# Two-layer hybrid streaming encoder: score rows of the sample requests gathered 64 wide, and the instruction order worked out with another model

## The chip, the cores and the metric

The kernel runs on one core of one Trainium2 chip, in one launch. The metric is the device time in microseconds of an execution. A core has five engines with a queue each, worked off in order: TensorE (PE in the profile; its weight loads are the rows PEld), VectorE (DVE), ScalarE (ACT), GpSimd (POOL) and SyncE (SP), which here only issues transfers.

## The reference, cut to what matters

Two layers, each with three mixers side by side (latent attention A, a gated recurrence B, differential attention C), sigmoid gates, an output projection and a gated MLP. The tokens are one prompt of 512 and eight sample requests of 16 tokens each, every request with a cache of 512 past keys. The change is in mixer C for the sample requests:

```python
s = einsum('bqhjd,bkhjd->bjhqk', qd, dk_all) * DF_SCALE   # j = 0, 1: two score maps per head
p = softmax(where(chunk_mask, s, NEG), axis=-1)
a = p[:, 0] - lam * p[:, 1]                                # 16 tokens x 8 heads, 528 keys
o_c = einsum('bhqk,bkhd->bqhd', a, dv_all)
o_c = rms(o_c, diff_norm_g) * (1 - lam_init)
```

Per request there are 2 maps x 8 heads x 16 tokens = 256 score rows over 512 cached and 16 new keys.

## The kernel before, in words

All is float32; the large products are split in a high and a low part of type fp32r and take three matmuls (`mm3`, L119 to L123). The 640 tokens are five tiles of 128. In a layer four Python generators are stepped in an order written out by hand, the string `ORDER`: `stream_a`, `stream_b`, `stream_c` for the mixers and `stream_g` for the gates. After them come the merge of the branches, the output projection and the MLP (up-projection, convolution, down-projection), without generators.

The stepping gives each instruction a place in the program. The Tile library then makes each engine's queue out of it: it runs the program on a model of the machine and hands an engine, when that model says it is free, the earliest instruction that the model says is ready. So work of one stream fills gaps of another: projections of `stream_g` and `stream_b` stand between the short steps of the attention and the recurrence. Which model is used is an argument of `tile.TileContext` in `build` (L1389). On the chip an engine keeps the order it was given.

Mixer C for the samples is one step per request b (eight per layer, sixteen in all):

- `c_probs(b)`. Four tiles of keys `kc` and four of values `vc` are loaded. For each block of two heads (`blk`, 0 to 3) four transposes (L831) and a copy give the keys `kT` with the features on the partitions, 128 x 512. `Qz` holds the queries of a block spread out with zeros, 32 columns per map j (two heads x 16 tokens). For each j one matmul (L835), 32 weight columns wide, fills 32 rows of `sc[j]`, so that `sc[0]` has map 0 of all heads and `sc[1]` map 1. A plain float32 matmul is two records in the trace. After that come the maximum, the exponential with row sums, and one operation over 128 x 640 (L850) that leaves `e[0] + c * e[1]`, c being minus lambda times the quotient of the row sums; the first row sum is divided out in the norm later.
- `c_out(b)`. Five transposes of `e[0]` (L857, L860) give the probabilities with keys on partitions, two copies take them to `at`, and 20 matmuls 32 columns wide (L866) multiply them with the values.

`c_probs(b + 1)` is put ahead of `c_out(b)`. The scores against the 16 new keys of all requests (L809) are made before the loop, 64 matmuls per layer.

The recurrence of `stream_b` has six levels per pair of heads, with four pairs per layer. A level is 8 to 10 short matmuls (L985), a masked copy on VectorE (L990), then products on GpSimd and VectorE (L995 to L998) that the matmuls of the next level read. L1006 is the closing level.

Of the kernel before, what the change touches and what calls it, by code (L numbers as in the profile page):

```python
# [12 lines left out]
ALU = mybir.AluOpType  # L13
# [40 lines left out]
def body(ctx: ExitStack, tc: tile.TileContext, i, o, depth=DEPTH):  # L54
# [132 lines left out]
    def constants():  # L187
        masks = C("masks", [128, len(LEVELS), 32], U8)
        mf = T("t", [128, len(LEVELS), 32])
        SY.dma_start(mf[:], i["c_masks"])  # L190
        V.tensor_copy(masks[:], mf[:])
        rope = C("rope", [128, 2, NT, 32])
        SY.dma_start(rope[:], i["c_rope"])
        hsel = C("hsel", [128, 2])
        SY.dma_start(hsel[:], i["c_hsel"])
        bsel = C("bsel", [128, NB])
        SY.dma_start(bsel[:], i["c_bsel"])
        half2 = C("half2", [128, 2])
        SY.dma_start(half2[:], i["c_half2"])
        identf = C("identf", [128, 64])  # L200
# [24 lines left out]
        for d in range(DEPTH):  # L225
            V.tensor_tensor(lbl[:, d], lbl[:, d], lmx[:], op=ALU.subtract)
            A.activation(lbl[:, d], lbl[:, d], AF.Exp)
            if d == 0:
                V.tensor_copy(lsm[:], lbl[:, 0])
            else:  # L230
                V.tensor_tensor(lsm[:], lsm[:], lbl[:, d], op=ALU.add)
        V.reciprocal(lsm[:], lsm[:])
        lbs = C("lbs", [128, DEPTH, 4])
        lb1 = C("lb1", [128, DEPTH, 4])
        lrun = C("lrun", [128, 4])
        for d in range(DEPTH):
# [7 lines left out]
        return masks, rope, hsel, bsel, half2, identf, Sbd, qz, lbs, lb1  # L244

    wz0 = []
    for l in range(depth):
# [408 lines left out]
        def stream_c():  # L656
# [9 lines left out]
            for t in range(NT):  # L666
                SY.dma_start(dst("p_dv", "s_dv", t), dv[t])
            dkn = T("pd", [128, 4, 128])
            Qz_t = T("ob", [128, 4, 2, NB, 2, NS])
            Qz = [Qz_t[:, blk] for blk in range(4)]  # L670
            parts = {}

# [5 lines left out]
            def c_inproj(u):  # L678

                w = wload2(W_in, C_DQ + u * 256)  # L680
                for c in range(2):
# [14 lines left out]
                    G.memset(Qz[blk].rearrange("p j b h n -> p (j b h n)"), 0.0)  # L696
                    for hh in range(2):
                        for j in range(2):
                            p0 = hh * 64 + j * 32
                            G.tensor_copy(Qz[blk][p0:p0 + 32, j, :, hh], dqn[p0:p0 + 32].rearrange("p (b n) -> p b n", b=NB))  # L700
                w = wload2(W_in, C_DK + u * 256)
                dkT = []
                for c in range(2):
# [97 lines left out]
            late()  # L801


            ps = P("tp")
            pv = ps[:, :256].rearrange("p (b j n) -> p b j n", b=NB, j=2)
            for b in range(NB):
                for j in range(2):
                    for blk in range(4):
                        PE.matmul(pv[32 * blk:32 * blk + 32, b, j], lhsT=Qz[blk][:, j, b], rhs=dkn[:, blk, b * NS:(b + 1) * NS],  # L809
                                  start=True, stop=True, tile_position=(0, 32 * blk))  # L810
            snew = C("snewc", [128, NB, 2, NS])
            V.tensor_copy(snew[:], pv)
            smx = C("smxc", [128, NB, 2])
            V.tensor_reduce(smx[:], snew[:], axis=AX.X, op=ALU.max)
            yield
            s0s = []

            def c_probs(b):
                if b % 4 == 0:
                    s0s.append(S1())  # L820
# [7 lines left out]
                for blk in range(4):  # L828
                    tp = P("tp")
                    for kt in range(4):  # L830
                        PE.transpose(tp[:, kt * 128:(kt + 1) * 128], kc[blk][:, kt], ident[:])  # L831
                    kT = T("a", [128, 512])
                    copy(kT[:], tp[:])
                    for j in range(2):
                        PE.matmul(sc[j][32 * blk:32 * blk + 32], lhsT=Qz[blk][:, j, b], rhs=kT[:], start=True, stop=True,  # L835
                                  tile_position=(0, 32 * blk))
                st = S1()
                e = [T("e", [128, 640]) for _ in range(2)]
                for j in range(2):
                    G.memset(e[j][:, 512:640], 0.0)  # L840
                    V.tensor_reduce(st[:, 6 + j:7 + j], sc[j][:], axis=AX.X, op=ALU.max)
                    V.tensor_scalar(st[:, j:j + 1], st[:, 6 + j:7 + j], smx[:, b, j:j + 1], -1.0, op0=ALU.max, op1=ALU.mult)
                    A.activation(e[j][:, 0:512], sc[j][:], AF.Exp, bias=st[:, j:j + 1], accum_out=st[:, 2 + j:3 + j])
                    A.activation(e[j][:, 512 + b * NS:528 + b * NS], snew[:, b, j], AF.Exp, bias=st[:, j:j + 1], accum_out=st[:, 4 + j:5 + j])
                s0 = s0s[b // 4][:, b % 4:b % 4 + 1]
                V.tensor_tensor(s0, st[:, 2:3], st[:, 4:5], op=ALU.add)
                V.tensor_tensor(st[:, 8:9], st[:, 3:4], st[:, 5:6], op=ALU.add)
                V.reciprocal(st[:, 9:10], st[:, 8:9])
                V.scalar_tensor_tensor(st[:, 10:11], st[:, 9:10], nlam, s0, op0=ALU.mult, op1=ALU.mult)
                V.scalar_tensor_tensor(e[0][:], e[1][:], st[:, 10:11], e[0][:], op0=ALU.mult, op1=ALU.add)  # L850
                return vc, e[0]

            def c_out(b, vc, e):
                at = T("a", [128, 640])
                tp = P("tp")
                for kt in range(4):
                    PE.transpose(tp[:, kt * 128:(kt + 1) * 128], e[:, kt * 128:(kt + 1) * 128], ident[:])  # L857
                copy(at[:, :512], tp[:])
                tp = P("tp")
                PE.transpose(tp[:, :128], e[:, 512:640], ident[:])  # L860
                copy(at[:, 512:640], tp[:, :128])
                ov = P("tp")
                for blk in range(4):
                    for kt in range(5):
# [7 lines left out]
            ahead = c_probs(0)  # L872
            for bh in range(2):
                ovs = T("t", [128, 4, 128])
                rs = s0s[bh]
# [14 lines left out]
                scaled_rstd(st[:, 8:12], 4, rs)  # L890
# [215 lines left out]
        for _ in range(2):  # L1106
            next(streams["A"])
        if l == 0:
            masks, rope, hsel, bsel, half2, identf, Sbd, qz, lbs, lb1 = constants()
# [250 lines left out]
def _consts():  # L1360
# [12 lines left out]
    for li, H in enumerate(LEVELS):  # L1373
# [2 lines left out]
    hsel = np.stack([hh == 0, hh == 1], 1).astype(np.float32)  # L1376
    bsel = (s[:, None] // 16 == np.arange(8)[None, :]).astype(np.float32)
    half2 = (0.5 * (s[:, None] // 64 == np.arange(2)[None, :])).astype(np.float32)
    return {"c_ident": np.eye(128, dtype=np.float32), "c_masks": masks, "c_rope": np.ascontiguousarray(rope, dtype=np.float32),
            "c_hsel": hsel, "c_bsel": bsel, "c_half2": half2}  # L1380


def build(shapes, depth=DEPTH):
# [2 lines left out]
    ins = {n: nc.dram_tensor(f"in_{n}_dram", a.shape, mybir.dt.from_np(a.dtype), kind="ExternalInput").ap()  # L1386
           for n, a in shapes.items()}
    outs = {n: nc.dram_tensor(f"out_{j}_dram", s, F32, kind="ExternalOutput").ap() for j, (n, s) in enumerate(_OUTS)}
    with tile.TileContext(nc) as tc:  # L1389
        body(tc, ins, outs, depth)  # L1390
    return nc

# [10 lines left out]
```

## Time and profile before

| | |
|---|---|
| three runs | 2873.95, 2877.69 (median), 2877.95 us |
| the profiled execution | 2880.15 us, its span 2878.3 us |
| mean granted TensorE clock | 0.988 |
| PE busy | 2799.7 us, 97% of the span |
| DVE, ACT, POOL busy | 51%, 35%, 12% |
| DMA, read and written | 245.37 MB and 44.09 MB, 101 GB/s over the span |

Busy shares count an engine's instructions and leave out its waits. The records of matmuls overlap, since they are pipelined: a record's duration is not what the next one has to wait. Where the trace prints a run of n records as one row, the row's length less one record's duration, over n - 1, is the distance from start to start.

### The profile page before, as it was taken

The numbers are of one execution on the slowest core, as the hardware profiler recorded it, in microseconds if no ns is written. First come the engines' busy times: TensorE is split into PE (matmuls) and PEld (weight loads), VectorE is DVE, ScalarE is ACT, GpSimd is POOL, SyncE is SP. The second block draws the span as 40 slices with busy tenths as digits, with TensorE's granted clock in tenths as the row PEclk, the third lists the DMA queues.
The fourth block names the chain that finished last, engine by engine and source line by source line (L and its number), as shares of the span: only waits on it lengthen the run. The fifth ranks groups of instructions, "written<-read, shape, count | busy, mean of one in ns | idle before, by whom it ended". The sixth has DMA issues, their size and how long they took to land. (4 is left out here: it accounts for less than half of the span.)

```text
span 2878.3 us, 48206 instructions
## 1 busy us (share of the span) xinstructions
PE 2799.7 (97%) x19408; PEld 2528.4 (88%) x19408; DVE 1469.0 (51%) x3085; ACT 1001.8 (35%) x2114; POOL 357.0 (12%) x583
## 2 busy tenths in 40 slices
PE   7999999999999999999999999999999999999998
PEld 7979997778889999998898799977798899999976
DVE  5465454355665544443454653633656645444444
ACT  4444453232222322223344543632322323222332
POOL 1000120012222010100000011200223211010000
PEclk9999999999999999999999999999999999999999
DMA  4213563424244122222233146444332542222222
GB/s 145 73 50 110 157 185 106 131 71 129 70 149 149 60 78 79 78 83 70 95 112 96 39 126 179 125 121 124 92 105 73 165 129 62 79 77 78 84 73 73
DMA packets 297994, 293.63 MB, mean 102 GB/s; under 512 B 51492, under 2 KB 254764, under 8 KB 296236
## 3 DMA queue, kind: packets, MB, share of 16 engines
q1 hardware_dynamic: 290092, 277.97, 31.8%
q0 software_dynamic: 7680, 12.59, 1.9%
q8 instruction: 153, 2.51, 0.4%
q14 instruction: 69, 0.57, 0.1%
HBM read 245.37 MB, written 44.09 MB: 101 GB/s over the span
## 5 line engine op out<-in xcount | busy, mean ns | idle before, releaser
L99 DVE TENSOR_TENSOR wl<-wr,wh 128x1024 fp32r<-128x1024 f32 (+2 forms) x292 | 371.2, 1272 | 345.4 <-ACT wh L98 342.2
L98 ACT CAST wh<-wr 128x1024 fp32r<-128x1024 f32 (+2 forms) x292 | 305.1, 1045 | 596.7 <-PE sc L123 229.2
L123 PE MATMUL mm<-xh,wh 128*128 128x320 f32 x1280 | 409.6, 320 | 0.0
L123 PE MATMUL sc<-ob,wh 128*128 128x320 f32 x1568 | 402.8, 311 | 5.6 <-DVE pd L1162 5.6
L123 PE MATMUL mm<-xl,wh 128*128 128x320 f32 x1280 | 407.7, 318 | 0.0
L123 PE MATMUL mm<-xh,wl 128*128 128x320 f32 x1280 | 406.9, 318 | 0.0
L123 PE MATMUL mm<-wh,xh 128*128 128x256 f32 (+1 forms) x960 | 279.2, 291 | 5.5 <-ACT xh L1168 2.7
L123 PEld LDWEIGHTS sc<-ob,wh 128*128 128x128 f32 x1568 | 276.5, 189 | 6.4 <-DVE pd L1162 6.2
L123 PE MATMUL mm<-wh,xl 128*128 128x256 f32 (+1 forms) x960 | 278.4, 290 | 1.4 <-DVE xl L99 1.0
L123 PE MATMUL mm<-wl,xh 128*128 128x256 f32 (+1 forms) x960 | 278.9, 291 | 0.0
L123 PE MATMUL mm<-ob,wh 128*128 128x320 f32 (+1 forms) x1088 | 275.1, 313 | 1.2 <-ACT ob L98 0.7
L123 PE MATMUL sc<-ob,wl 128*128 128x320 f32 x832 | 259.0, 311 | 0.0
L123 PEld LDWEIGHTS mm<-xh,wl 128*128 128x128 f32 x1280 | 243.7, 190 | 5.8 <-issue 3.7
L123 PEld LDWEIGHTS mm<-xh,wh 128*128 128x128 f32 x1280 | 244.1, 191 | 3.9 <-issue 1.5
L123 PEld LDWEIGHTS mm<-xl,wh 128*128 128x128 f32 x1280 | 243.8, 190 | 3.2 <-issue 0.4
L123 PE MATMUL mm<-ob,wl 128*128 128x320 f32 (+1 forms) x720 | 224.6, 312 | 0.0
L123 PEld LDWEIGHTS mm<-ob,wh 128*128 128x128 f32 x1088 | 189.4, 188 | 2.9 <-DVE ob L99 1.1
L123 PEld LDWEIGHTS mm<-wh,xh 128*128 128x128 f32 x960 | 181.8, 190 | 8.3 <-ACT wh L98 3.7
L123 PE MATMUL sc<-pd,wh 128*128 128x320 f32 x608 | 188.9, 311 | 0.0
L123 PEld LDWEIGHTS mm<-wh,xl 128*128 128x128 f32 x960 | 181.7, 189 | 3.7 <-issue 1.6
L123 PEld LDWEIGHTS mm<-wl,xh 128*128 128x128 f32 x960 | 181.9, 190 | 1.3 <-issue 0.8
L123 PEld LDWEIGHTS sc<-ob,wl 128*128 128x128 f32 x832 | 157.3, 189 | 0.0
(389 smaller groups left out, 5192.5 us busy)
## 6 DMA issues: line engine op xcount, KB each, us to landing
wr<-in_w_in_dram SPq DMA_DIRECT2D x104, 512.0 KB, 4.1
wr<-in_ffn_w_up_dram SPq DMA_DIRECT2D x88, 512.0 KB, 3.6
wr<-in_ffn_w_down_dram SPq DMA_DIRECT2D x44, 512.0 KB, 3.8
pd<-in_cache_diff_k_dram SPq DMA_DIRECT2D x64, 256.0 KB, 4.1
pd<-in_cache_diff_v_dram SPq DMA_DIRECT2D x64, 256.0 KB, 3.2
gp<-g SPq DMA_DIRECT2D x48, 320.0 KB, 3.0
pd<-gp SPq DMA_DIRECT2D x48, 320.0 KB, 3.4
wr<-in_w_branch_dram SPq DMA_DIRECT2D x24, 512.0 KB, 4.2
```

The lines of the kernel that those rows point to most:

```text
L98: a = A.copy(hi, src)
L99: v = V.tensor_tensor(lo, src, hi.bitcast(F32), op=ALU.subtract)
L123: PE.matmul(out, lhsT=a, rhs=b, start=(j == 0), stop=(j == n - 1))
```

## The change

Four edits.

1. `Qz` is laid out with the maps next to each other, so that a block's 64 queries (2 maps x 2 heads x 16 tokens) are 64 neighbouring columns. One matmul per block, 64 columns wide, takes the place of two of 32. Block `blk` fills half of the rows of `sc[blk // 2]`. The scores with the new keys are gathered in the same way.
2. The two maps of a head now stand in rows of one tile, so `e[0]` and `e[1]` can't be combined row by row. Instead a constant 128 x 64 selection matrix `sel`, whose rows for map 1 are scaled by minus lambda once per layer (`selc`), is scaled by the reciprocals of the row sums (`sw`), and the matmul that turns the probabilities picks the rows, scales and adds them: 10 plain matmuls in `c_out` (5 key tiles x 2) in place of 5 transposes. L850 goes, and both tiles of `e` are read by `c_out`.
3. The probabilities come out divided by their sums, so the norm no longer gets `rs` and leaves out its extra products.
4. `schedule_with_timeline_sim=True`: the order on every engine, in the whole program, comes from the library's timeline model in place of the model used so far.

```diff
-            Qz_t = T("ob", [128, 4, 2, NB, 2, NS])
+            Qz_t = T("ob", [128, 4, NB, 2, 2, NS])
...
+            def qrows(blk, b):
+                return Qz[blk][:, b].rearrange("p j h n -> p (j h n)")
...
             for b in range(NB):
-                for j in range(2):
-                    for blk in range(4):
-                        PE.matmul(pv[32 * blk:32 * blk + 32, b, j], lhsT=Qz[blk][:, j, b], rhs=dkn[:, blk, b * NS:(b + 1) * NS],
-                                  start=True, stop=True, tile_position=(0, 32 * blk))
+                for blk in range(4):
+                    r0 = 64 * (blk % 2)
+                    PE.matmul(pv[r0:r0 + 64, b, blk // 2], lhsT=qrows(blk, b), rhs=dkn[:, blk, b * NS:(b + 1) * NS],
+                              start=True, stop=True, tile_position=(0, r0))
...
+            selc = C("selc", [128, 64])
+            st = S1()
+            V.scalar_tensor_tensor(st[:, 0:1], sel[:, 65:66], nlam, sel[:, 64:65], op0=ALU.mult, op1=ALU.add)
+            V.tensor_scalar(selc[:], sel[:, 0:64], st[:, 0:1], None, op0=ALU.mult)
...
-                    for j in range(2):
-                        PE.matmul(sc[j][32 * blk:32 * blk + 32], lhsT=Qz[blk][:, j, b], rhs=kT[:], start=True, stop=True,
-                                  tile_position=(0, 32 * blk))
+                    r0 = 64 * (blk % 2)
+                    PE.matmul(sc[blk // 2][r0:r0 + 64], lhsT=qrows(blk, b), rhs=kT[:], start=True, stop=True, tile_position=(0, r0))
...
-                s0 = s0s[b // 4][:, b % 4:b % 4 + 1]
-                V.tensor_tensor(s0, st[:, 2:3], st[:, 4:5], op=ALU.add)
-                V.tensor_tensor(st[:, 8:9], st[:, 3:4], st[:, 5:6], op=ALU.add)
-                V.reciprocal(st[:, 9:10], st[:, 8:9])
-                V.scalar_tensor_tensor(st[:, 10:11], st[:, 9:10], nlam, s0, op0=ALU.mult, op1=ALU.mult)
-                V.scalar_tensor_tensor(e[0][:], e[1][:], st[:, 10:11], e[0][:], op0=ALU.mult, op1=ALU.add)
-                return vc, e[0]
+                V.tensor_tensor(st[:, 8:10], st[:, 2:4], st[:, 4:6], op=ALU.add)
+                V.reciprocal(st[:, 10:12], st[:, 8:10])
+                for q in range(2):
+                    V.tensor_scalar(sw[:, q], selc[:], st[:, 10 + q:11 + q], None, op0=ALU.mult)
+                return vc, e, sw
...
-                for kt in range(4):
-                    PE.transpose(tp[:, kt * 128:(kt + 1) * 128], e[:, kt * 128:(kt + 1) * 128], ident[:])
-                copy(at[:, :512], tp[:])
-                tp = P("tp")
-                PE.transpose(tp[:, :128], e[:, 512:640], ident[:])
-                copy(at[:, 512:640], tp[:, :128])
+                for k0, k1 in ((0, 4), (4, 5)):
+                    tp = P("tp")
+                    for kt in range(k0, k1):
+                        for q in range(2):
+                            c0 = (kt - k0) * 128 + q * 64
+                            PE.matmul(tp[:, c0:c0 + 64], lhsT=e[q][:, kt * 128:(kt + 1) * 128], rhs=sw[:, q], start=True, stop=True)
+                    copy(at[:, k0 * 128:k1 * 128], tp[:, :(k1 - k0) * 128])
...
-    with tile.TileContext(nc) as tc:
+    with tile.TileContext(nc, schedule_with_timeline_sim=True) as tc:
```

## Rows read from the trace of the kernel before

**Rows 1.** The page: span, and busy time, share and count of each engine.

```profile
span 2878.3 us, 48206 instructions
PE 2799.7 (97%) x19408; PEld 2528.4 (88%) x19408; DVE 1469.0 (51%) x3085; ACT 1001.8 (35%) x2114; POOL 357.0 (12%) x583
```

**Rows 2.** Windows: stretch, its length, busy us (count) by engine, clock, DMA share, GB/s.

```profile
0.00:50.00 50.00, 32.48 (x184) 30.07 (x184) 25.62 (x59) 22.35 (x45) 6.28 (x17) 0.97 0.52 161
...
300.00:456.00 156.00, 152.17 (x1102) 146.02 (x1101) 86.68 (x278) 80.50 (x217) 32.45 (x60) 0.98 0.56 156
456.00:640.00 184.00, 183.15 (x1368) 133.66 (x1357) 75.27 (x167) 55.54 (x134) 11.11 (x21) 1.00 0.37 107
640.00:846.00 206.00, 194.21 (x1625) 177.74 (x1624) 127.27 (x246) 58.32 (x109) 55.49 (x58) 0.97 0.37 110
...
1720.00:1880.00 160.00, 152.22 (x1166) 145.99 (x1167) 85.67 (x273) 80.44 (x214) 32.43 (x60) 0.98 0.54 152
1880.00:2050.00 170.00, 169.81 (x1156) 121.28 (x1145) 63.20 (x139) 52.03 (x129) 5.83 (x16) 1.00 0.39 111
2050.00:2275.00 225.00, 212.58 (x1807) 195.11 (x1806) 142.84 (x276) 63.45 (x117) 63.96 (x64) 0.97 0.35 106
...
2715.00:2879.00 164.00, 152.08 (x651) 121.48 (x649) 70.26 (x92) 51.79 (x80) 2.76 (x5) 0.97 0.23 78
```

**Rows 3.** Groups of instructions: busy us, mean ns of one, idle before.

```profile
L835 PE MATMUL sc<-a,ob 128*32 128x512 f32 x256 | 105.7, 598 | 0.2
...
L784 PE MATMUL ov<-ob,a 128*128 128x64 f32 x320 | 46.0, 276 | 0.0
...
L784 PEld LDWEIGHTS ov<-ob,a 128*128 128x128 f32 x320 | 41.6, 192 | 5.8 <-ACT a L782 4.0
...
L850 DVE SCALAR_TENSOR_TENSOR e<-e,st,e 128x640 f32<-128x640 f32 x16 | 14.1, 881 | 0.7
```

**Rows 4.** Timeline of PE in one step of the sample scores.

```profile
484.40 2.57 PE L835 MATMUL sc<-a,ob 128*32 128x512 f32 x8
486.91 1.09 PE L831 MATMUL tp<-ident,pd 128*128 128x128 f32 x8
...
488.28 1.90 PE L835 MATMUL sc<-a,ob 128*32 128x512 f32 x4
490.12 0.66 PE L857 MATMUL tp<-ident,e 128*128 128x128 f32 x4
...
490.82 1.90 PE L835 MATMUL sc<-a,ob 128*32 128x512 f32 x4
492.66 0.33 PE L860 MATMUL tp<-ident,e 128*128 128x128 f32 x1
```

**Rows 5.** Timeline of PE: 128 x 128 weights with 64 moving columns.

```profile
415.61 0.64 PE L784 MATMUL ov<-ob,a 128*128 128x64 f32 x4
...
417.86 1.00 PE L784 MATMUL ov<-ob,a 128*128 128x64 f32 x8
```

**Rows 6.** Timeline of PE: scores with new keys, then levels of the recurrence.

```profile
455.69 1.27 PE L809 MATMUL tp<-pd,ob 128*32 128x16 f32 x128
...
668.59 0.81 PE L985 MATMUL sc<-qz,pd 128*64 128x64 f32 x20 [0.94 <-DVE pd L996]
...
672.14 0.80 PE L985 MATMUL sc<-qz,pd 128*64 128x64 f32 x20 [0.93 <-DVE e L998]
...
677.36 0.69 PE L985 MATMUL sc<-qz,pd 128*64 128x64 f32 x16
...
679.58 0.69 PE L985 MATMUL sc<-qz,pd 128*64 128x64 f32 x16
```

**Rows 7.** Who waited for the last transpose, L860: us in total, times.

```profile
  POOL e L840: 172.3, 12
```

More of the change, by code (lines that the diff above doesn't have):

```diff
@@ L199, in constants @@
         SY.dma_start(half2[:], i["c_half2"])
+        sel = C("sel", [128, 66])
+        SY.dma_start(sel[:], i["c_sel"])
         identf = C("identf", [128, 64])
@@ L243, in constants @@
             V.tensor_scalar(lb1[:, d], lbs[:, d], -1.0, 1.0, op0=ALU.mult, op1=ALU.add)
-        return masks, rope, hsel, bsel, half2, identf, Sbd, qz, lbs, lb1
+        return masks, rope, hsel, bsel, half2, sel, identf, Sbd, qz, lbs, lb1
     wz0 = []
@@ L695, in c_inproj @@
                     c_park(blk, "q", 1, ql[:])
-                    G.memset(Qz[blk].rearrange("p j b h n -> p (j b h n)"), 0.0)
+                    G.memset(Qz[blk].rearrange("p b j h n -> p (b j h n)"), 0.0)
                     for hh in range(2):
@@ L699, in c_inproj @@
                             p0 = hh * 64 + j * 32
-                            G.tensor_copy(Qz[blk][p0:p0 + 32, j, :, hh], dqn[p0:p0 + 32].rearrange("p (b n) -> p b n", b=NB))
+                            G.tensor_copy(Qz[blk][p0:p0 + 32, :, j, hh], dqn[p0:p0 + 32].rearrange("p (b n) -> p b n", b=NB))
                 w = wload2(W_in, C_DK + u * 256)
@@ L801, in stream_c @@
             late()
+            def qrows(blk, b):
+                return Qz[blk][:, b].rearrange("p j h n -> p (j h n)")
             ps = P("tp")
-            pv = ps[:, :256].rearrange("p (b j n) -> p b j n", b=NB, j=2)
+            pv = ps[:, :256].rearrange("p (b q n) -> p b q n", b=NB, q=2)
             for b in range(NB):
-                for j in range(2):
-                    for blk in range(4):
-                        PE.matmul(pv[32 * blk:32 * blk + 32, b, j], lhsT=Qz[blk][:, j, b], rhs=dkn[:, blk, b * NS:(b + 1) * NS],
-                                  start=True, stop=True, tile_position=(0, 32 * blk))
+                for blk in range(4):
+                    r0 = 64 * (blk % 2)
+                    PE.matmul(pv[r0:r0 + 64, b, blk // 2], lhsT=qrows(blk, b), rhs=dkn[:, blk, b * NS:(b + 1) * NS],
+                              start=True, stop=True, tile_position=(0, r0))
             snew = C("snewc", [128, NB, 2, NS])
@@ L833, in c_probs @@
                     copy(kT[:], tp[:])
-                    for j in range(2):
-                        PE.matmul(sc[j][32 * blk:32 * blk + 32], lhsT=Qz[blk][:, j, b], rhs=kT[:], start=True, stop=True,
-                                  tile_position=(0, 32 * blk))
+                    r0 = 64 * (blk % 2)
+                    PE.matmul(sc[blk // 2][r0:r0 + 64], lhsT=qrows(blk, b), rhs=kT[:], start=True, stop=True, tile_position=(0, r0))
                 st = S1()
                 e = [T("e", [128, 640]) for _ in range(2)]
[L839 to L844, printed above, removed]
@@ L853, in c_out @@
-            def c_out(b, vc, e):
-                at = T("a", [128, 640])
-                tp = P("tp")
-                for kt in range(4):
-                    PE.transpose(tp[:, kt * 128:(kt + 1) * 128], e[:, kt * 128:(kt + 1) * 128], ident[:])
-                copy(at[:, :512], tp[:])
-                tp = P("tp")
-                PE.transpose(tp[:, :128], e[:, 512:640], ident[:])
-                copy(at[:, 512:640], tp[:, :128])
+                sw = C("sw", [128, 2, 64], bufs=2)
+                for q in range(2):
+                    G.memset(e[q][:, 512:640], 0.0)
+                    V.tensor_reduce(st[:, 6 + q:7 + q], sc[q][:], axis=AX.X, op=ALU.max)
+                    V.tensor_scalar(st[:, q:q + 1], st[:, 6 + q:7 + q], smx[:, b, q:q + 1], -1.0, op0=ALU.max, op1=ALU.mult)
+                    A.activation(e[q][:, 0:512], sc[q][:], AF.Exp, bias=st[:, q:q + 1], accum_out=st[:, 2 + q:3 + q])
+                    A.activation(e[q][:, 512 + b * NS:528 + b * NS], snew[:, b, q], AF.Exp, bias=st[:, q:q + 1], accum_out=st[:, 4 + q:5 + q])
@@ new lines, in c_probs, with c_out @@
+                V.tensor_tensor(st[:, 8:10], st[:, 2:4], st[:, 4:6], op=ALU.add)
[3 more added lines that the diff above has]
+                return vc, e, sw
+            def c_out(b, vc, e, sw):
+                at = T("a", [128, 640])
+                for k0, k1 in ((0, 4), (4, 5)):
+                    tp = P("tp")
+                    for kt in range(k0, k1):
+                        for q in range(2):
+                            c0 = (kt - k0) * 128 + q * 64
+                            PE.matmul(tp[:, c0:c0 + 64], lhsT=e[q][:, kt * 128:(kt + 1) * 128], rhs=sw[:, q], start=True, stop=True)
+                    copy(at[:, k0 * 128:k1 * 128], tp[:, :(k1 - k0) * 128])
@@ L874, in stream_c @@
                 ovs = T("t", [128, 4, 128])
-                rs = s0s[bh]
                 for b4 in range(4):
@@ L889, in stream_c @@
                 V.scalar_tensor_tensor(st[:, 8:12], sv[:, :, 1], hsel[:, 1:2], st[:, 8:12], op0=ALU.mult, op1=ALU.add)
-                scaled_rstd(st[:, 8:12], 4, rs)
+                scaled_rstd(st[:, 8:12], 4, None)
                 on = T("t", [128, 4, 128])
@@ L1108, in body @@
         if l == 0:
-            masks, rope, hsel, bsel, half2, identf, Sbd, qz, lbs, lb1 = constants()
+            masks, rope, hsel, bsel, half2, sel, identf, Sbd, qz, lbs, lb1 = constants()
         lam = C("lam", [128, 8])
@@ L1378, in _consts @@
     half2 = (0.5 * (s[:, None] // 64 == np.arange(2)[None, :])).astype(np.float32)
+    r = (s // 64, s // 32 % 2, s // 16 % 2, s % 16)
+    c = np.arange(64)
+    sel = ((r[0][:, None] == c // 32) & (r[2][:, None] == c // 16 % 2) & (r[3][:, None] == c % 16)).astype(np.float32)
+    sel = np.concatenate([sel, (r[1] == 0)[:, None], (r[1] == 1)[:, None]], 1).astype(np.float32)
     return {"c_ident": np.eye(128, dtype=np.float32), "c_masks": masks, "c_rope": np.ascontiguousarray(rope, dtype=np.float32),
-            "c_hsel": hsel, "c_bsel": bsel, "c_half2": half2}
+            "c_hsel": hsel, "c_bsel": bsel, "c_half2": half2, "c_sel": sel}
 def build(shapes, depth=DEPTH):
```

3 lines of the change are left out of this document (removed).

## Prediction

> **What bounds the kernel now.** The page comes first: PE is busy for 2799.7 of 2878.3 us, the next engine, DVE, for half of the span [rows 1]. Then the windows, to see whether that holds in the stage that the change rewrites. It does: between 456 and 640 us PE is busy for 183.15 of 184 us, in the second layer for 169.81 of 170, at a granted clock of 1.00, with DVE and ACT idle more than half of the time [rows 2]. So a microsecond of PE work less in that stage is a microsecond less in the kernel as long as other matmuls fill its gaps, and work taken from DVE is worth nothing there. The rest of the windows tells what an order could still win. PE stands idle for 78.6 us in all. Of that 17.5 us fall in the first 50 us and 11.9 us in the last 164, where there is little to reorder. 36 us fall in four windows: two with the prompt's scores and averages (3.8 and 7.8) and two with the recurrence (11.8 and 12.4) [rows 2]. The last look is at single PE rows of a step of the sample scores, to price what goes and comes.
>
> **The scores, 64 columns wide.** Before, L835 has 256 records and keeps PE for 105.7 us [rows 3]. A block's four records take 1.90 us, so one starts 0.43 us after the other, with one record's 0.60 us [rows 3] at the end. Where two blocks stand together, eight records take 2.57 us instead of the 3.6 us that this distance would give: neighbours that fill different columns of the array overlap, those of the same columns don't [rows 4]. A step is one such eight and two fours, 6.4 us, and 16 steps make 102 us. After it a block is two records, 0.43 + 0.60 = 1.03 us. The pair that stands together takes from 1.03 (both halves of the array side by side) to 1.90 us (one after the other). A step is then 3.1 to 4.0 us. I take 3.3, near the lower end, since the eight overlapped as far as its order let it: 53 us in all, **-49 us**. The ends are -39 (no overlap) and -70 (every pair side by side, 32 pairs at 1.03 us).
>
> The Trainium skill, "TensorEngine Tiling (Array Packing)", section Key Properties, says that tiles work independently and that different tiles can load weights and multiply in parallel; the trace agrees only for neighbours in the queue, by the 2.57 us above. By that rule alone the scores would take the 32 x 1.03 = 33 us of the far end.
>
> **The turn of the probabilities.** It was five transposes a step, 0.66 + 0.33 = 0.99 us [rows 4]. It becomes ten plain float32 matmuls with 128 weight columns and 64 moving ones, 20 records. The trace has this shape elsewhere: L784, eight records in 1.00 us and four in 0.64 [rows 5], so 0.10 to 0.12 us from start to start and 0.28 for the last one [rows 3]. A run of 16 takes 0.28 + 15 x 0.103 = 1.83 us, one of four 0.64, together 2.5 us. So 1.5 us more a step, **+25 us** for 16. The lower end is +22, with every record at 0.103 us. At the upper end the weight loads, 192 ns each [rows 3], are not hidden: 20 x 0.192 = 3.8 us a step, +46. I take +25, since L784 does hide them.
>
> **The scores with the new keys.** L809 has 128 records a layer in 1.27 us [rows 6]. It becomes 64 records with 64 weight columns on alternating halves. The nearest row is the recurrence's L985, 20 in 0.81 us, which is 0.03 us a record [rows 6]: 2.2 us, **+2 us** for both layers, between 0 and +5.
>
> **What lies beside PE.** L850 goes, 16 x 0.88 us of DVE [rows 3], and in come two products of 64 columns a step, less than that. The norm loses a few tiny operations, and one small constant is loaded. All of it lies in stages where DVE is busy 75 of 184 us [rows 2]: 0 us. If PE's filler were gone, the shorter chain would give back up to the 14 us of L850. A wait is lengthened: `e[1]` was free after L850 and is now held until the matmuls of `c_out` have read it. The memset on POOL (L840) that opens the next `e` waits for it. It waits like this already for `e[0]`, twelve times, 172.3 us in all, for the last transpose [rows 7]. So the slot comes free at the same place of the program as the one that POOL waits for now. Behind it in POOL's queue stand gate sums and recurrence products, and PE passes over these with projections; POOL is busy for 11 of 184 us. I take 0; at worst each of the 16 waits exposes the step's 0.9 us of extra matmul time, +15.
>
> The sum of the edits to the arithmetic is -49 + 25 + 2 = **-22 us**.
>
> **The order.** No row of the trace shows the other model's queues, so I bound it. Below, it can at best give back the idle time of the four uneven windows, -36 us. Above, it can take away cover: in the recurrence, levels start 2.2 to 3.6 us apart while a level's matmuls take 0.7 to 0.8 us [rows 6]; the rest, about 1.6 us on average, is filled with projections of other streams. There are 6 levels and the closing one, 4 pairs, 2 layers: 56 such gaps, some 90 us of cover. Dependencies, buffers and durations are the same under both models, and nothing in the rows says which one fills better. I take 0, nearest to the row that says 97% busy, with ends at -36 and +90.
>
> So the profiled execution's 2880.15 us (span 2878.3) becomes 2858. The median of the runs shown, 2877.69, lies 2.5 us below that execution, so the forecast for the median is **2856 us**.
>
> **Rivals.**
>
> *The order wins as well.* For it speaks that the four windows are uneven: the recurrence waits for DVE at 668 and 672 us with 0.9 us each [rows 6], though projections were to be had. Against it, the stage of the sample scores has nothing left to win. With half to all of the 36 us: 2838 to 2820.
>
> *The halves of the array run side by side throughout.* The new order would have to put each pair's two matmuls together; now one pair of two in a step stands so [rows 4]. Then -70 in place of -49: 2835.
>
> *The order uncovers the recurrence: slower.* The model lets PE run through the projections of `stream_g` and `stream_b` early, in the stages where it finds them ready, so that fewer are left for the 56 gaps. Each gap without filler costs 1.6 us. The 22 us that the matmuls give are used up at 14 gaps, a quarter; from 18 on the kernel is slower beyond doubt. Half of the gaps: 2856 + 45 = 2901 us. For it speaks that these windows are already the least filled [rows 2] and that `ORDER` deals the projections out by hand; against it, that the order of the steps still sets the priorities.
>
> *The order costs about what the matmuls give.* 10 to 17 gaps or as much at the seams of the stages: 2872 to 2883, no change.
>
> *The matmuls don't give it.* If the weight loads of the turn are bare (+46), the arithmetic gives -49 + 46 + 2 = -1, no change either; L784 speaks against it.
>
> **How the numbers follow.** The forecast, with the order worth within 10 us either way: 0.38, with a range of its own from 2840 to 2868. The order wins: 0.22. Side by side throughout: 0.05. No change, by either way: 0.12. Recurrence uncovered: 0.23. About 0.2% (5.8 us) is what runs of this kernel can tell from no change. Faster is 0.38 + 0.22 + 0.05 = 0.65, same 0.12, slower 0.23. The range that leaves out 2 in 10 reaches from 2818 (all idle time of the four windows given back) to 2900 (half of the gaps bare).
>
> **What would show it.** The score matmuls should have 128 records and be busy for 50 to 60 us; the turn, 320 records and some 40 us; the new keys' scores, 128 records. Busy PE should fall by about 20 us, and if PE's idle time stays near 78 us, the order was worth nothing. The windows of the recurrence tell the rest: PE idle well over 12 us a layer, with levels waiting for DVE or POOL and no projections between them, is the slower case; under 6 us, the case in which the order wins. The prediction is wrong if busy PE doesn't fall, or if the idle time moves by more than the matmuls give.

## The result, and the profile after

The changed kernel takes 2925.93 us (median of 4 runs, 2924.04 to 2927.64) against 2875.82 us for the kernel before on the same chip: a ratio of 1.0174 [1.016, 1.0188], 50 us slower. The forecast was 2856 us, its range ended at 2900 us. Times are medians; one execution of e2 (14123 us) and one of e3 (3174 us) were slow and are left out of the ratios, and without them the medians are 2948.07 and 2917.75 us.

The page of the kernel after (span, busy time and count by engine, to be set beside [rows 1]):

```profile
span 2924.3 us, 48196 instructions
PE 2808.8 (96%) x19392; PEld 2571.5 (88%) x19392; DVE 1483.3 (51%) x3057; ACT 1001.1 (34%) x2114; POOL 340.7 (12%) x583
```

PE has fewer records and is busy for longer, and its idle time (span less busy time) has grown from 78.6 to 115.5 us. The mean granted clock fell from 0.988 to 0.973. Windows of the kernel after show where (columns as in [rows 2]):

```profile
245.00:300.00 55.00, 50.25 (x339) 42.61 (x338) 32.42 (x70) 26.49 (x69) 4.72 (x14) 1.00 0.33 91
...
300.00:456.00 156.00, 155.03 (x1130) 153.40 (x1129) 86.35 (x255) 75.80 (x201) 33.91 (x60) 1.00 0.61 171
456.00:640.00 184.00, 181.34 (x1379) 147.01 (x1377) 79.78 (x186) 64.48 (x159) 12.96 (x25) 1.00 0.38 109
...
800.00:870.00 70.00, 49.15 (x320) 41.88 (x316) 34.88 (x72) 13.29 (x24) 15.82 (x17) 0.68 0.23 70
870.00:1000.00 130.00, 127.62 (x967) 127.03 (x966) 70.40 (x112) 34.43 (x51) 24.97 (x20) 1.00 0.41 128
...
2240.00:2310.00 70.00, 47.40 (x335) 40.74 (x335) 37.23 (x79) 12.84 (x24) 15.49 (x17) 0.68 0.26 80
```

The stage of the prompt's scores, 300 to 456 us, is fuller than before (idle 1.0 us, before 3.8). The largest hole stands at the end of the recurrence: 70 us with 21 and 23 us idle, at a clock of 0.68, once in each layer (800 and 2240 us). A smaller hole is in the sample requests of the latent attention (245 to 300 us, 4.75 us idle). The last pair of the recurrence in PE's timeline:

```profile
814.85 1.34 PE L989 MATMUL sc<-qz,pd 128*64 128x64 f32 x20 [2.17 <-DVE a L994]
817.99 1.12 PE L989 MATMUL sc<-qz,pd 128*64 128x64 f32 x16 [1.80 <-DVE pd L1000]
820.65 1.12 PE L989 MATMUL sc<-qz,pd 128*64 128x64 f32 x16 [1.54 <-DVE pd L1000]
823.30 1.94 PE L1010 MATMUL sc<-qz,pd 128*64 128x128 f32 x8 [1.53 <-DVE pd L1000]
826.52 1.11 PE L1036 MATMUL tp<-ident,pd 128*128 128x128 f32 x4 [1.27 <-DVE pd L1025]
```

No projection stands between the levels. PE waits for DVE before each one, and the 20 records take 1.34 us where they took 0.81 [rows 6], because the clock is at its lower level (1.2 GHz). The projections that stood there before are not gone: they were issued earlier. PE's queue is the same in every run, so the projection matmuls (L123) between neighbouring levels can be counted in it. For a layer, the counts between the six levels of a pair of heads; the numbers between bars stand between two pairs:

```
before  13 11 12 14 12 | 48 | 11 11 10 10  9 | 463 |  6 13 15 16  9 | 35 | 15 16 11 10 9
after   35 29 26 30 28 | 92 |  0  0 28 32 26 | 301 | 32 29 29 27 28 | 44 |  0  0  0  0 0
```

The other model puts 26 to 35 projections into a gap where the model before put 6 to 16, and then has none left: seven gaps a layer are bare of projections, two in the second pair and all five in the last. With the two gaps around the closing level, which the forecast counted as well, the last pair has seven bare gaps and the layer nine.

The groups of the score matmuls and of the turn (busy us, mean ns of one; L835 of [rows 3] is now L842):

```profile
L842 PE MATMUL sc<-a,ob 128*64 128x512 f32 x128 | 66.5, 618 | 2.3 <-DVE a L95 1.3 <-ACT a L93 1.0
...
L865 PE MATMUL tp<-sw,e 128*128 128x64 f32 x320 | 41.9, 278 | 0.0
```

### The profile page after: what moved, and what is told of

Read it like the earlier page. It is cut to its first block, busy times and chain, and to the rows that moved or that the text cites. A ratio compares the mean times of both kernels' runs of the same rounds, so it can differ in the third digit from the quotient of the medians.

```text
span 2924.3 us, 48196 instructions
## 1 busy us (share of the span) xinstructions
PE 2808.8 (96%) x19392; PEld 2571.5 (88%) x19392; DVE 1483.3 (51%) x3057; ACT 1001.1 (34%) x2114; POOL 340.7 (12%) x583
## 4 chain that ended last, share of the span: by engine, by line
PE 90%; DVE 5%; ACT 2%; DMA 1%; issue 1%; POOL 0%; SPq 0%; DVEq 0%; POOLq 0%; ACTq 0%
PE mm L123 42%; PE sc L123 17%; PE sc L842 2%; PE sc L1294 2%; PE sc L1295 2%; PE sc L1296 2%; PE tp L871 2%; PE mm L1296 1%; PE mm L1295 1%; PE mm L1294 1%; PE tp L865 1%; PE tp L636 1%; PE sc L554 1%; PE sc L989 1%; PE ov L786 1%
## 5 line engine op out<-in xcount | busy, mean ns | idle before, releaser
L99 DVE TENSOR_TENSOR wl<-wr,wh 128x1024 fp32r<-128x1024 f32 (+2 forms) x292 | 377.3, 1294 | 285.5 <-ACT wh L98 282.9
L123 PE MATMUL sc<-ob,wh 128*128 128x320 f32 x1568 | 403.3, 312 | 12.3 <-DVE pd L1166 12.3
L123 PE MATMUL mm<-xh,wh 128*128 128x320 f32 x1280 | 407.2, 318 | 3.0 <-DVE pd L939 3.0
L123 PE MATMUL mm<-xh,wl 128*128 128x320 f32 x1280 | 401.5, 314 | 0.6 <-DVE wl L99 0.6
L123 PE MATMUL mm<-xl,wh 128*128 128x320 f32 x1280 | 399.3, 312 | 0.0
L123 PEld LDWEIGHTS sc<-ob,wh 128*128 128x128 f32 x1568 | 277.2, 190 | 15.2 <-DVE pd L1166 12.7
L123 PE MATMUL mm<-wh,xh 128*128 128x256 f32 (+1 forms) x960 | 280.5, 293 | 6.6 <-ACT wh L98 3.0
L123 PE MATMUL mm<-ob,wh 128*128 128x320 f32 (+1 forms) x1088 | 280.0, 315 | 0.0
L123 PE MATMUL mm<-wl,xh 128*128 128x256 f32 (+1 forms) x960 | 278.9, 292 | 0.3 <-DVE wl L99 0.3
L123 PE MATMUL mm<-wh,xl 128*128 128x256 f32 (+1 forms) x960 | 279.2, 291 | 0.0
L123 PE MATMUL sc<-ob,wl 128*128 128x320 f32 x832 | 251.2, 311 | 0.0
L123 PEld LDWEIGHTS mm<-xh,wh 128*128 128x128 f32 x1280 | 240.8, 188 | 8.7 <-DVE pd L939 3.8
L123 PEld LDWEIGHTS mm<-xl,wh 128*128 128x128 f32 x1280 | 240.7, 188 | 4.2 <-issue 2.4
L123 PEld LDWEIGHTS mm<-xh,wl 128*128 128x128 f32 x1280 | 240.6, 188 | 3.8 <-issue 1.5
L123 PE MATMUL mm<-ob,wl 128*128 128x320 f32 (+1 forms) x720 | 224.0, 313 | 0.0
L123 PEld LDWEIGHTS mm<-ob,wh 128*128 128x128 f32 x1088 | 192.5, 190 | 0.7
L123 PEld LDWEIGHTS mm<-wh,xh 128*128 128x128 f32 x960 | 183.2, 191 | 8.6 <-ACT wh L98 5.7
L123 PE MATMUL sc<-pd,wh 128*128 128x320 f32 x608 | 189.0, 311 | 0.0
L123 PEld LDWEIGHTS mm<-wh,xl 128*128 128x128 f32 x960 | 183.5, 191 | 1.8 <-issue 1.6
L123 PEld LDWEIGHTS mm<-wl,xh 128*128 128x128 f32 x960 | 183.0, 191 | 1.3 <-DVE wl L99 0.8
L123 PEld LDWEIGHTS sc<-ob,wl 128*128 128x128 f32 x832 | 155.6, 189 | 0.0
```

Source lines behind the costliest of these rows:

```text
L99: v = V.tensor_tensor(lo, src, hi.bitcast(F32), op=ALU.subtract)
L123: PE.matmul(out, lhsT=a, rhs=b, start=(j == 0), stop=(j == n - 1))
```

## The experiments

The runs were made on several chips, on which the kernel before took 2871.6 to 2877.3 us. Where two runs with different values of it are compared, the number in brackets is the difference after each has been set against the kernel before beside it.

**The edits alone, the order alone.** e1_edits_only is the kernel after without the last edit; e2_order_only is the kernel before with that edit and no other. The edit of e1, against the kernel after:

```diff
-    with tile.TileContext(nc, schedule_with_timeline_sim=True) as tc:
+    with tile.TileContext(nc) as tc:
```

> The changed kernel with the order worked out as before: edits 1 to 3 alone. Theory (the new order is the loss, by using up the filler of the recurrence before the last pair of heads): the edits alone are faster. In this order 30 of the 32 pairs of score matmuls stand next to each other, so the scores should fall from 105.7 us busy to 33 to 42, the turn costs 28 us more (38 us in the changed kernel's trace against 10 before), the sum is -38 us: 2838 us, between 2828 and 2856; the recurrence's windows stay as before, some 12 us of idle PE a layer. Rival (the edits themselves cost: the turn, or the longer hold of the two probability tiles): 2890 us or more, no faster than before in any case.

> The kernel before with the timeline model's order alone: edit 4 without the rest. Theory: all of the loss and more, since the edits' gain is missing: 2926 + 11 = 2937 us (2925 to 2952), with the last pair of heads of each layer bare of projections, about 20 us of idle PE and a granted clock near 0.7 there. Rival (the edits cost, the order is neutral): 2876 us.

e1 took 2847.75 us, 0.9921 [0.9906, 0.9936] of before: -24. e2 took 2948.23 us, 1.0261 [1.0243, 1.0278]: +76. Both lie within the ranges expected of them. So the sum of the edits to the arithmetic, forecast at -22, came out to 2 us, and the order, taken at 0, cost 76 us without the edits and 78 with them (2925.93 less 2847.75) [74]. The page of e1:

```profile
span 2844.2 us, 48127 instructions
PE 2761.3 (97%) x19392; PEld 2540.7 (89%) x19392; DVE 1455.6 (51%) x3057; ACT 996.5 (35%) x2110; POOL 359.8 (13%) x583
```

Against the kernel after it has as many PE records, 47.5 us less busy PE and 32.6 us less idle time. The recurrence of e1, as a window and its last pair's levels in PE's timeline:

```profile
640.00:822.00 182.00, 170.71 (x1479) 157.62 (x1479) 112.88 (x217) 52.96 (x98) 46.65 (x47) 0.99 0.36 107
```

```profile
777.54 0.80 PE L989 MATMUL sc<-qz,pd 128*64 128x64 f32 x20 [0.40 <-DVE pd L1000]
780.58 0.80 PE L989 MATMUL sc<-qz,pd 128*64 128x64 f32 x20 [0.43 <-DVE e L1002]
783.17 0.69 PE L989 MATMUL sc<-qz,pd 128*64 128x64 f32 x16
785.38 0.69 PE L989 MATMUL sc<-qz,pd 128*64 128x64 f32 x16
```

The clock stays at 0.99, and the levels have their cover: 6 to 20 projections in each gap.

**Is it the cover?** Three runs. e5_fill_early leaves the kernel before as it is but for the string `ORDER`, in which the last two steps of the gates come four steps of the recurrence earlier, so that the last two pairs of each layer are bare:

```diff
-ORDER = "...BBGBGBBBBBBBBGG"
+ORDER = "...BBGBGBBBBGGBBBB"
```

> The kernel before, order worked out as before, with one change in the string ORDER: the last two gate steps stand ahead of the last two pairs of heads of the recurrence, so that their 192 projection matmuls a layer are spent and both pairs run bare. Theory (what costs time is a recurrence without filler, by whichever model): each bare pair costs what the bare pair of the timeline order costs, about 16 us of idle PE and 8 us of half clock, so 2 pairs x 2 layers x 24 = 96 us more: 2968 us, between 2930 and 2995. Rival (the bare pair of the timeline order is a symptom, its time is lost elsewhere): under 2890 us.

It took 2942.88 us, 1.0246 [1.023, 1.0261]: +70, 17.6 us for each of the four bare pairs: less than the 96 expected, but inside the range and far over the rival. The windows of its two holes look like those of the kernel after, without the other model:

```profile
800.00:880.00 80.00, 56.83 (x417) 48.75 (x415) 44.44 (x98) 15.29 (x30) 21.31 (x26) 0.69 0.20 58
...
2250.00:2330.00 80.00, 57.04 (x428) 49.23 (x425) 44.42 (x97) 15.29 (x30) 21.80 (x26) 0.68 0.20 60
```

So 70 us can be lost by nothing but the place of the filler. PE idles for 23 us in each hole of two pairs, 11.5 us a pair; the rest of the price goes with the lower clock (last section). The other two runs try to put it back in the kernel after. e3_hold_gate holds the matmuls of the last gate step behind the first level of the last pair:

```diff
-            next(streams[ch], None)
+            steps_g += ch == "G"
+            if ch == "G" and steps_g == 12:
+                with tc.issue_after(kept[3, 0].ins):
+                    next(streams[ch], None)
+            else:
+                next(streams[ch], None)
```

> The changed kernel, timeline order, but the projections of the last gate step (96 matmuls, 14 us a layer) may not be issued before the first level of the last pair of heads. Theory: the last pair gets filler again (20 to 30 matmuls in each of three gaps), idle PE there falls from 21 to under 10 us a layer and the clock stays higher: 2895 us (2880 to 2908). Rival (the time is lost elsewhere, and the matmuls that are held leave a hole of the same size in the pair before): 2926 us, within 8.

It took 2918.37 us, 1.0159 [1.0141, 1.0176]; 8 us [4] less than the kernel after: the theory missed and its rival held. The count in PE's queue tells why: pair 4 now has 24, 21, 29, 22, 0 between its levels, but pair 3 has 32, 29, 29, 3, 0, and none stands between the two pairs, where there were 44. The model still issues what is ready in bunches of some 30; the hole moved to the pair before. e7_spread_rec therefore deals out the 192 matmuls of the last two gate steps by the dozen, each dozen behind its own level of pairs 3 and 4, the last two behind the closing level:

```diff
+            if hold:
+                n = len(prs) // hold[0]
+                for j0 in range(0, len(prs), n):
+                    with tc.issue_after(hold[1].pop(0).ins):
+                        for j in range(j0, j0 + n):
+                            PE.matmul(ps[:, :HT], lhsT=prs[j][0], rhs=prs[j][1], start=(j == 0), stop=(j == len(prs) - 1))
...
+                if steps_g in (11, 12):
+                    kept["hold", 1, steps_g - 9] = (2, [kept[steps_g - 9, min(j, 6)] for j in range(8)])
```

> The changed kernel, timeline order, with the 192 projection matmuls of the last two gate steps tied in dozens to the levels of the last two pairs of heads: none of a dozen is issued before its level. The order then has 12 in each gap, where it had some 30 a gap in one pair and none in the other. Theory (the timeline model fills a gap with 30 matmuls, 4.4 us, where the chain needs less than 2 us, and so runs out; the hold on one step alone left holes in the pair before): about 16 us of idle PE and 7 us of half clock come back per layer: 2880 us, between 2866 and 2895. Rival (as with the one step held): no lower than 2912 us.

It took 2904.13 us, 1.0108 [1.0093, 1.0124], 22 us [19] less than the kernel after: between theory and rival. The window of its recurrence,

```profile
740.00:850.00 110.00, 94.89 (x739) 85.07 (x740) 66.44 (x132) 27.47 (x53) 26.12 (x29) 0.86 0.32 97
```

has 15 us idle and a clock of 0.86: better than the hole, not yet the 0.99 of e1. All seven gaps of the last pair are covered now; pair 3, which had some 30 projections a gap, is down to 12.

**The second place.** In the kernel after, no projection stands between the short steps of the latent attention's sample requests (7 L123 matmuls a step, all of the attention's own; 18 to 43 before). Before, the stretch of these steps had next to no idle time:

```profile
226.00:284.00 58.00, 57.96 (x405) 52.30 (x404) 33.73 (x71) 30.42 (x75) 3.94 (x11) 1.00 0.32 88
```

One such step of the kernel after in PE's timeline:

```profile
253.34 0.50 PE L123 MATMUL sc<-t,qrs 96*128 96x512 f32 x1 [0.36 <-DVE t L343]
...
257.25 0.66 PE L600 MATMUL tp<-ident,pd 128*128 128x128 f32 x4 [0.24 <-ACT ob L93]
...
258.46 0.61 PE L605 MATMUL tp<-ident,krc 128*32 128x128 f32 x4 [0.23 <-DVE pd L99]
```

Every step waits three times, 0.8 us together. e8_spread_att holds the four projections of the second gate step behind the scores of requests 0 to 3, in the way of e7; e9_spread_both does both.

```diff
+                if steps_g == 2:
+                    kept["hold", 0, 1] = (1, [kept["a", b] for b in (0, 1, 2, 3)])
```

> The changed kernel, timeline order, with the four projections of the second gate step (96 matmuls a layer) each held until the scores of sample requests 0, 1, 2, 3 of the latent attention. In the timeline order these steps have 7 matmuls each and no projection; now four of them get 24 more. Theory: the second place where filler was spent too early gives back 10 to 14 us a layer: 2900 us, between 2888 and 2912. Rival (the gaps of the attention steps come from the order of its own work): 2926 us, within 8.

> The changed kernel, timeline order, with both spreads, the recurrence's and the attention's. Theory: both gains add up, 46 + 26 us: 2854 us, between 2838 and 2872, near the edits alone with the old order (2848 us). Rival (there is a third place, or the one gain eats the other): over 2885 us.

e8 took 2913.68 us, 1.0145 [1.013, 1.016]: -12 [-9], less than expected and just outside its range, which ended at 2912. e9 took 2890.32 us, 1.0066 [1.0049, 1.0082]: -36 [-32], about the sum of the two (-34 [-28]). Both places are real and add up, and the two are not all: 43 us [42] to e1 are left, as the rival of e9 had it.

**The third place: the pairs.** In e1 30 of the 32 pairs of score matmuls stand next to each other in PE's queue, in the kernel after 2. Its step of the scores in the timeline:

```profile
550.91 1.07 PE L842 MATMUL sc<-a,ob 128*64 128x512 f32 x2 [0.35 <-DVE a L95]
551.91 0.66 PE L838 MATMUL tp<-ident,pd 128*128 128x128 f32 x4
552.50 1.07 PE L842 MATMUL sc<-a,ob 128*64 128x512 f32 x2
```

Each block's two records stand alone, 1.07 us, parted by the transposes of the next keys. Two pairs in e1:

```profile
522.74 1.40 PE L842 MATMUL sc<-a,ob 128*64 128x512 f32 x4
...
525.68 1.27 PE L842 MATMUL sc<-a,ob 128*64 128x512 f32 x4
```

Four records in 1.40 and 1.27 us, where two take 1.07. The 30 pairs of e1 take from 1.08 to 1.91 us, half of them 1.63 or more. Whether it is the halves of the array that overlap, e4_same_half asks: e1 with the blocks in an order that makes the first two and the last two of a step fill the same half.

```diff
-                for blk in range(4):
+                for blk in (0, 2, 3, 1):
```

> Edits 1 to 3 alone, in the order as before, with the blocks of a step taken as 0, 2, 3, 1 in place of 0, 1, 2, 3: neighbours in the queue then fill the same half of the array, and of 30 pairs that differ in their half 6 are left. Same instructions, same sizes. If different halves run side by side: 24 pairs lose 0.85 us each, 20 us more than the edits alone (15 to 25), and the scores are busy some 20 us longer. Rival (neighbours on different halves gain nothing): the time of the edits alone, within 4 us.

It took 2862.83 us, 0.9966 [0.9953, 0.9979]: 15 us over e1, of the expected sign and at the low end. The groups of e1 and of e4 agree with the time, 49.8 and 63.7 us:

```profile
L842 PE MATMUL sc<-a,ob 128*64 128x512 f32 x128 | 49.8, 628 | 0.1
...
L865 PE MATMUL tp<-sw,e 128*128 128x64 f32 x320 | 39.7, 277 | 0.1
```

```profile
L842 PE MATMUL sc<-a,ob 128*64 128x512 f32 x128 | 63.7, 619 | 0.1
```

But the edit did more than was meant: it also parted the blocks. In e4's queue 36 of the 64 blocks stand alone (4 in e1), 8 pairs of neighbours fill the same half and take 1.93 to 2.30 us, 6 fill different halves and take 1.40 to 1.57. Most of the 14 us of busy time, some 10, comes from the blocks that stand alone, so the time of e4 alone doesn't settle the question. One step does, the first of the second layer, in e1 and then in e4; in both the copy of the second block's keys (L93) ends 0.1 us after the first matmul has started:

```profile
1865.25 0.58 ACT L93 COPY a<-tp 128x512 f32<-128x512 f32 x1 [3.61 <-PE tp L838]
...
1865.73 1.26 PE L842 MATMUL sc<-a,ob 128*64 128x512 f32 x4
```

```profile
1877.78 0.58 ACT L93 COPY a<-tp 128x512 f32<-128x512 f32 x1 [3.42 <-PE tp L838]
...
1878.26 2.30 PE L842 MATMUL sc<-a,ob 128*64 128x512 f32 x4
```

Different halves take 1.26 us, the same half 2.30: there the second matmul starts only after both records of the first have started.

e10_pairs puts the pairs together under the other model: e9, with both blocks' keys made first and the first matmul of a pair held until the second block's keys have been copied.

```diff
+                        if blk % 2 == 0:
+                            tc.add_manual_dep(m_.ins, cps[1].ins.name, ...)
```

> The changed kernel, timeline order, both spreads, and each pair of score matmuls kept together: the first of a pair also waits for the keys of the second, and all 32 pairs stand next to each other in the order, where it was 2. Theory (the third place of the loss: the timeline order parted the pairs, 66.5 us busy against 49.8): 14 us less than both spreads, 2876 us, between 2868 and 2883. Rival (the wait costs what the overlap gives): 2890 us, within 5.

It took 2855.94 us, 0.9943 [0.9924, 0.9962]: 34 us [33] less than e9, where 14 were expected. The group and two pairs in the timeline say where the rest came from:

```profile
L854 PE MATMUL sc<-a,ob 128*64 128x512 f32 x128 | 34.5, 618 | 0.0
```

```profile
524.48 1.08 PE L854 MATMUL sc<-a,ob 128*64 128x512 f32 x4
...
527.81 1.08 PE L854 MATMUL sc<-a,ob 128*64 128x512 f32 x4
```

A pair now takes 1.08 us, as long as one block alone. In e9 the group took 68.6 us, so 34.1 us went. To be neighbours in the queue was not enough in e1, where 33 to 42 us had been expected of the group and 49.8 were measured: the second matmul waited for its keys while the first ran, and only what was left overlapped. The trace of e1 shows that wait: where the copy of the second block's keys ends after the first matmul has started, the second starts 0.05 us after the end of the copy. The Trainium skill, "TensorEngine Tiling (Array Packing)", section Key Properties, says that different tiles can load weights and multiply in parallel. The trace agrees once both are ready when the first starts (1.08 against 1.07 us).

**The turn, and a better version.** e6_transposes prices the ten matmuls of the turn: e1 with five transposes of `e[0]` in their place. It leaves out the rows of the last four heads, `e[1]`, and the weights of the two maps.

> Edits 1 to 3 alone, old order, with the turn made by five transposes of the first probability tile as before, in place of the ten plain matmuls (so the second tile's rows and the weights of the maps are left out of the output). What the turn costs by itself: in the edits alone its matmuls are busy 39.8 us, the five transposes 16 us before. Theory (PE is the bound there, its work counts in full): 24 us less than the edits alone, 2824 us, between 2816 and 2832. Rival (the turn lies beside other work): 2848 us, within 5.

It took 2825.26 us, 0.9833 [0.9814, 0.9852]: 22.5 us less than e1, so the turn costs that much, forecast +25. If so, transposes may be the cheaper way even where there are ten of them. e11_scaled_rows is e1 with the whole computation: each row of `e` is scaled on DVE by its factor (the reciprocal sum, for map 1 times minus lambda), ten transposes follow, and the two maps are added as they are copied out.

```diff
-                    V.tensor_scalar(sw[:, q], selc[:], st[:, 10 + q:11 + q], None, op0=ALU.mult)
+                    V.tensor_scalar(e[q][:], e[q][:], st[:, 10 + q:11 + q], lrow[:], op0=ALU.mult, op1=ALU.mult)
...
-                            PE.matmul(tp[:, c0:c0 + 64], lhsT=e[q][:, kt * 128:(kt + 1) * 128], rhs=sw[:, q], start=True, stop=True)
+                        PE.transpose(tp[:, kt * 128:(kt + 1) * 128], e[q][:, kt * 128:(kt + 1) * 128], ident[:])
+                    A.copy(av[:, 0:4, q], tv[:, :, :, 0])
+                    V.tensor_tensor(av[:, 0:4, q], av[:, 0:4, q], tv[:, :, :, 1], op=ALU.add)
```

> A version meant to beat both: edits 1 and 3, old order, and another turn. The rows of both tiles are scaled by the reciprocal sum, map 1 also by minus lambda (one DVE product over 640 columns a tile), ten transposes turn them, and the evictions add the halves of the two maps (a copy on ACT, a sum on DVE). Ten transposes at 0.11 us are 1.1 us a step in place of 2.3: if PE is the bound, 18 us less than the edits alone, 2830 us, between 2820 and 2840. Rival (the extra work on DVE and ACT, some 1.5 us a step, or the longer chain to the averages shows): 2848 us or more.

2828.33 us, 0.9845 [0.9823, 0.9868]: 19 us less than e1, as expected. e12_best adds the pairs of e10 and keeps the old order; in e11 22 of the 32 pairs stand together, and the scores are busy for 53.2 us.

> The scaled rows with the turn by transposes, old order, and each pair of score matmuls kept together by letting the first wait for the second's keys as well. In the old order 30 of 32 pairs were neighbours without that, yet the scores are busy for 53 us there and for 34.5 where the pairs are kept together. Theory (being next in the queue is not enough: the second has to be ready when the first starts): the scores fall to 35 us and the time by as much, 18 us: 2810 us, between 2803 and 2818. Rival (what the kept pairs won under the timeline order was the order's own, and here the first of a pair now waits in front of ready work): 2828 us or more.

2812.68 us (median of 5), 0.9772 [0.9755, 0.9789]: 65 us less than before, 16 us [21] less than e11, and faster than any other kernel here. Its two groups, the scores and the larger part of the turn:

```profile
L843 PE MATMUL sc<-a,ob 128*64 128x512 f32 x128 | 34.5, 618 | 0.2
...
L866 PE MATMUL tp<-ident,e 128*128 128x128 f32 x128 | 19.3, 279 | 0.0
```

## Why the prediction was wrong, step by step

**The order, "I take 0".** This is the step that failed, by 74 to 78 us. With the order of before the other terms stood, but for the scores', which was 7 us too small (below). I took the value "nearest to the row that says 97% busy", but a row of the kernel before says how well one model fills, nothing about the other. The bounds (-36, +90) held it; the choice between them was not worked out. The rival "the order uncovers the recurrence" named mechanism and place, and why: the model runs through projections where it finds them ready and leaves none for later. In the kernel after 9 of the forecast's 28 gaps per layer are bare, 18 in all, the number from which the rival called the kernel slower beyond doubt; at the forecast 1.6 us they make 29 us. e7 covered the seven of the last pair in each layer and gave back 22 us [19], 1.3 to 1.6 us each, while it thinned the pair before. In e5 a bare gap cost 2.5 us (17.6 us over seven), of which at most 1.6 us are PE's idle time: the price was right for the wait and left out the clock.

Where the rival stopped short: there were two more places. The holes of the latent attention were worth 12 us [9] (e8). And the parted pairs, which I had only as a chance of a gain (0.05), turned into a loss: 66.5 us for the group in place of 49.8, 17 us. Together 22 + 12 + 17 = 51 of the 78 us [45 of 74]. Some 27 us [29] stay open. e10, which has all three repairs, says much the same: with better pairs than e1 (34.5 against 49.8 us) it should be at 2832 and is at 2856. Its mean clock is 0.982 against 0.99 in e1, and between 640 and 822 us PE is idle for 18 us at a clock of 0.92, in e1 for 11 us at 0.99: the recurrence, whose first pair still gets 24 to 29 matmuls a gap. Nor is PE's the only queue that the other model wrote. In the merge of the branches, right behind the recurrence, PE waits for DVE, whose queue has other work first. The wait in the kernel after, in e10 and in e1 (total us, times, longest):

```profile
PE sc L123 <- DVE pd L1166: 12.3, 2, 6.1
```

```profile
PE sc L123 <- DVE pd L1187: 12.3, 2, 6.1
```

```profile
PE sc L123 <- DVE pd L1166: 7.1, 5, 3.1
```

So up to 5 us of the rest may belong to DVE's order, which the repairs left to the model; no run tests it, nor the remainder.

**The scores, -49.** In busy time 105.7 to 49.8, -56, with the order of before: inside the bounds of -39 and -70, 7 us more than forecast (49.8 in place of 53, and the forecast set out from 102 in place of 105.7). Under the new order it was 66.5, -39, the end without overlap. The far end, 33 us for the group, was reached as well, 34.5 us in e10 and e12, by a condition that I hadn't thought of: both matmuls ready before the first starts. The profile of before had shown a half of it, "one pair of two in a step stands so" [rows 4].

**The turn, +25.** In busy time 39.7 against 11.25 + 4.92 us for L857 and L860 before: +23.5 in e1. Removing it gave 22.5 (e6). L784 was the right row. (The forecast's own rows add up to +24, with a lower end of about +20, in place of +25 and +22.) With the new keys' scores, +1.7 in busy time (2.54 to 4.25), the three terms make -31 in e1. The time fell by 24, so some 7 us of that didn't come through, and it is in part luck that the sum came so close to -22.

**What lies beside PE, 0.** The loss needs nothing from it: e1 has every one of these edits and came out near the sum. The lengthened hold of `e[1]` was not tried alone.

**The signs named.** "PE idle well over 12 us a layer, with levels waiting for DVE or POOL and no projections between them" is what the windows at 800 and 2240 us show, 21 and 23 us. Busy PE, which was to fall by 20 us, rose by 9, and the idle time grew by 37: both were named as signs of being wrong. The group of the scores missed its 50 to 60 us (66.5), which is the parted pairs. The one sign that I hadn't named was the clock.

## What to carry to other kernels

An edit that changes who writes the instruction order is a change of the whole program: it can't be entered at zero because the present order is full, and it is cheap to run alone. Filler is worth something by where it stands; count it between the steps of each serial chain, and deal it out evenly, since a chain that had used up its filler paid twice here, in idle time and in clock. Two narrow matmuls on different halves of the array cost here as much as one (1.08 against 1.07 us), if both had their operands when the first started; to keep them together was worth 16 to 34 us (e12 against e11, e10 against e9).

## What the runs showed of the hardware

The clock was not in the sum. In the kernel after PE worked in short bursts at the end of the recurrence, with waits of mostly 1 to 2 us between them, and was busy for 70% of the window at 800 us; the granted clock there was 0.68. A level of 20 records then takes 1.34 us in place of 0.81. That is a second price of a bare gap beside the wait itself: in e5 a bare pair cost 17.6 us, where seven gaps at the forecast 1.6 us make 11. The clock has two levels, 1.2 and 2.4 GHz, so that 2 x (1 - clock) x span is the time at the lower one: 69 us in the kernel before, 57 in e1, 158 in the kernel after. Of the 80 us by which the span of the kernel after exceeds that of e1, 33 are idle time and 17 the parted pairs. The other 30 are busy time; an estimate from the 101 us more at the lower level, of which at most half is lost, is that the clock can account for them.
